# Conv taps queued behind the last low half, copies shared by two engines, later loads of x and fewer pairs by seven in a hybrid decoder layer

## The chip, the cores and the metric

The kernel runs on one core of a Trainium2 chip. The metric is the device time of one execution in microseconds. TensorE (PE) does matmuls, VectorE (DVE) and ScalarE (ACT) elementwise work, GpSimd (POOL) little here; SyncE (SP) issues the loads. The weights stream from HBM through the whole run.

## The reference

One layer on x (256 x 4096) and 256 memory tokens: a projection of x by w_in, whose columns feed three groups, each gated; the groups together go through w_out, and a layer norm closes the layer.

```python
proj = x @ w_in[l]
(c_a, c_b, c_gate, g_q, g_k, g_v, g_lr, g_gate, m_q, m_gate) = jnp.split(proj, split_idx, axis=-1)
y_conv = _conv_group(c_a, c_b, ...) * silu(c_gate)     # h = c_a * sigmoid(c_b); 31-tap causal
                                                       # conv per channel; layer norm; silu
y_gla = _gla_group(g_q, g_k, g_v, g_lr, ...) * silu(g_gate)
y_mem = _memory_group(m_q, mem @ w_mem_kv[l]) * silu(m_gate)
out = concatenate([y_conv, y_gla, y_mem], axis=-1) @ w_out[l]
x = _layernorm(DN_ALPHA * x + out, ln_g[l], ln_b[l])
```

## The kernel before

**Products.** The data is float32; each operand is split into a high half (a cast on ScalarE, L122) and a low half (a subtraction on VectorE, L123) by `halves` (L120). A product takes three matmuls: high by high, high by low, low by high. The halves of x stay in SBUF (`hx`, `lx`); those of the weights (`hiw`, `low`) are made from each loaded chunk (`raww`) just ahead of use. The raw chunks have a ring of three, the halves rings of four tiles; `push` makes a tile and uses the one that was made three tiles earlier.

**Stages, in the order of the run.** Two pairs of conv projections (`cb`, each with its `ca`; about 6 to 97 and 97 to 202 us), memory keys and values (`memory`, L1036, 64 half tiles of 12 matmuls, 202 to 376), the memory queries (`mq`, to 460), two panels of GLA queries (to 550), the keys (`k`, to 632), the values, two pairs of gates (`gg`; the second from 893 to 976), the conv gates (`cg`, to 1062), the memory gates, then the output projection and the norm.

**Pairs by seven.** `pair` (L369) projects onto 1024 columns in 16 chunks of two k-tiles. A chunk by eight makes two tiles of 12 matmuls. A chunk by seven saves one product in eight: VectorE first makes differences of the weights, `tx` (L439) and `ty` (L445, L448), and then four tiles (c, a, y, x) of 3, 6, 6 and 6 matmuls follow. It also needs sums of the halves of x (`sums`, L175: one add L180, five small ones L190, and the halves `eh`, `el`). `BY7` (L50) gives for each pair the pattern of chunks, the blocks of x taken by seven, which sums are made after it is queued, and which are given back.

**Work between the tiles.** After a tile's matmuls `use` first takes one step of `later` (the adds that close the pair before), then `work` (transposes, sums, scores, by `do_work`) and `fill`. In `fill` are the conv's taps (`queue_conv`, L811; the 31 taps of 8 blocks of channels, each one VectorE instruction of 128 x at most 256, L828 and L837): after a pair's chunk as many as `FILLS` says (1 in the second conv pair, else 3), after a half tile of memory `MEM_FILLS` = 5. A transpose (`queue_transpose`, L221) is one VectorE instruction and 16 copies of 32 x 256 on ScalarE (L243). `X_AT` (L32) says with which chunk of the first pair which block of x is loaded; the loads stand with those of the weights on SP's queue.

The order in the code isn't that of the engines: the Tile framework simulates the program and places an instruction on its engine when its operands are ready. A tap needs only the conv's input and the tap ahead of it.

Of the kernel before, what the change touches and what calls it, by code (L numbers as in the profile page):

```python
# [9 lines left out]
F32 = mybir.dt.float32  # L10
# [3 lines left out]
ALU = mybir.AluOpType  # L14
# [5 lines left out]
KT = D // P  # L20
# [10 lines left out]

X_AT = {0: (1,), 1: (2,), 3: (3,), 4: (6,), 5: (4,), 6: (7,), 7: (5,)}  # L32

# [17 lines left out]
    ("cb", 0): ("8888888887878787", (6, 7), (), ()),  # L51
    ("cb", 1): ("8888878787878787", (5, 6, 7), (5,), (5,)),
    ("mq", 0): ("8888888887878787", (6, 7), (), (6, 7)),
    ("k", 0): ("8888878787878787", (5, 6, 7), (5, 6, 7), (5,)),
# [4 lines left out]

FILLS = {("cb", 1): 1}  # L60
MEM_FILLS = 5


@with_exitstack
def layer_kernel(ctx, tc, xT, memT, xres, w_mem, w_in, w_pairs, w_last, cst, w_gate,
                 conv_g, conv_b, norm_g, ln_g, ln_b, out):
    nc = tc.nc
# [52 lines left out]
    def halves(src, hi, lo):  # L120

        nc.scalar.copy(out=hi, in_=src)  # L122
        nc.vector.tensor_tensor(out=lo, in0=src, in1=hi.bitcast(F32), op=ALU.subtract)  # L123

# [34 lines left out]
    work = deque()  # L159
    fill = deque()  # L160
# [60 lines left out]
    def queue_transpose(src, dst, then, back=False):  # L221
# [11 lines left out]
        def moves(b):  # L233
            if b == 0:
                st["d"] = dst()
            tok = "p t (q j c) -> p t q j c"
            feat = "p q (t i c) -> p t q i c"
            flat = "p (q t i c) -> p t q i c" if back else "p (t q j c) -> p t q j c"
            sizes = dict(q=4, t=2, c=32)
            frm = st["t"].rearrange(flat, **sizes)  # L240
            to = st["d"].rearrange(tok if back else feat, c=32, **({"q": 4} if back else {"t": 2}))
            for a in range(4):
                nc.scalar.copy(  # L243
                    out=to[32 * b : 32 * b + 32, :, :, a, :],
                    in_=frm[32 * a : 32 * a + 32, :, :, b, :],
                )
# [48 lines left out]
    def flush():  # L295
        while stream:
            stream.popleft()()


    def panel(chunks, width, stat, then, fills=0, apart=0, soon=KT // 2):  # L300
# [20 lines left out]
        def make(c):  # L321
            if c % 2 == 0:
                raw[0] = w_raw([P, 4, width], "w")
                nc.sync.dma_start(
                    out=raw[0], in_=chunks[c // 2].rearrange("p (k n) -> p k n", k=4)
                )
            w = w_tiles([P, 2, width], "w", KT // 2 - apart <= c < KT // 2 - WBUFS)
            halves(raw[0][:, 2 * (c % 2) : 2 * (c % 2) + 2, :], *w)
            held[c] = w

        def use(c):
# [4 lines left out]
            if c < KT // 2 - apart:  # L336
                for w in held[c]:
                    for tt in range(2):
                        mms(c, tt, w, w is held[c][1])
            if later:  # L340
                later.popleft()()
            do_work(-(-len(work) // max(1, soon - c)))
            for _ in range(min(fills, len(fill))):
                fill.popleft()()

# [23 lines left out]
    def pair(chunks, order, stat, ext, then, soon=KT // 2, fills=0, units=False, beside=None):  # L369
# [41 lines left out]
        def make(n, i):  # L411
# [43 lines left out]
            w = tuple(t[:, : 1 if nm == "c" else 2, :] for t in w_tiles([P, 2, 512], "w"))  # L455
            halves(st[n][nm], *w)
            st[n, nm] = w
# [5 lines left out]
        def use(n, i):  # L463
# [10 lines left out]
            for second in range(2):  # L474
                for j, (slot, stationary, bk) in enumerate(terms):
                    sh, sl = stationary(c)
                    for s in (sh,) if second else (sh, sl):
# [6 lines left out]
                        )  # L484
            if later:
                later.popleft()()
            if i == len(tiles) - 1:
                for _ in range(min(fills, len(fill))):
                    fill.popleft()()
                do_work(-(-len(work) // max(1, soon - n)))  # L490

# [544 lines left out]
    def memory():  # L1036
        m_units, raws, tiles, banks = [], {}, {}, []

        def make(kt, half):
# [8 lines left out]
            tiles[kt, half] = w_tiles([P, 1024], "wm")  # L1048
            halves(raw, *tiles[kt, half])

        def use(kt, half):
# [22 lines left out]
            if half and kt % 4 == 3:  # L1074
                give(mh, ml)
            if later:
                later.popleft()()
            do_work(-(-len(work) // max(1, KT - kt)))
            for _ in range(min(MEM_FILLS, len(fill))):
                fill.popleft()()  # L1080

# [421 lines left out]
```

## Time and profile before

| | |
|---|---|
| time, median of 3 runs | 1538.81 us (1537.97 to 1539.09) |
| the profiled execution | 1540.91 us, of which the span is 1538.9 |
| mean granted TensorE clock | 0.993 of full speed |
| TensorE busy | 1506.4 us (98% of the span), 6809 matmuls |
| VectorE busy | 1210.9 us (79%) |
| ScalarE busy | 901.6 us (59%) |
| chain of work that ended last | TensorE 86%, VectorE 6%, ScalarE 3%, issue 3%, DMA 2% |

Busy time is the time in which an engine had at least one instruction under way; instructions overlap a little, so two starts lie closer together than one instruction is long. The span runs from the first to the last instruction. The granted clock is a share of full speed (2.4 GHz); the lower level is 1.2 GHz.

### The profile page before, as it was taken

What the parts mean: (1) busy time and instruction counts of PE and PEld (TensorE: products, weight loads), DVE (VectorE), ACT (ScalarE), POOL (GpSimd) and SP (SyncE); (2) the same over time, 40 slices, a digit from 0 to 9 for tenths busy, and PEclk for the clock granted to TensorE, in tenths of its full rate; (3) what the DMA queues carried; (4) which work ended last, traced back from release to release, by engine and by line L of the source; (5) the groups of instructions that cost most, each with busy time, mean ns of one, the idle gap of its engine ahead of it and who ended that gap; (6) DMA issues with size and microseconds to landing.
All of it is one profiled execution on the core that took longest, in us unless ns stands there. A gap on an engine that the chain in (4) does not pass through costs nothing.

```text
span 1538.9 us, 18500 instructions
## 1 busy us (share of the span) xinstructions
PE 1506.4 (98%) x6809; PEld 1265.8 (82%) x6809; DVE 1210.9 (79%) x1454; ACT 901.6 (59%) x1203; POOL 49.2 (3%) x59
## 2 busy tenths in 40 slices
PE   8999899999999999999999999999999999999997
PEld 6787678888888888899999887888888887888885
DVE  7799999997686579957575788887757589998955
ACT  6565357438668855676464468577685454555541
POOL 0000000000000000003030000000000000000001
PEclk9999999999999999999999999999999999999998
DMA  8564557765555465555445454656567545565662
GB/s 326 204 219 154 182 172 252 244 206 213 207 189 179 144 238 187 201 197 176 161 156 198 174 213 164 219 218 233 212 219 274 205 178 205 209 216 203 225 223 109
DMA packets 54515, 311.73 MB, mean 203 GB/s; under 512 B 6100, under 2 KB 6484, under 8 KB 27928
## 3 DMA queue, kind: packets, MB, share of 16 engines
q1 hardware_dynamic: 54424, 310.55, 57.1%
q8 instruction: 53, 0.87, 0.2%
q14 instruction: 38, 0.31, 0.1%
HBM read 304.24 MB, written 6.29 MB: 202 GB/s over the span
## 4 chain that ended last, share of the span: by engine, by line
PE 86%; DVE 6%; ACT 3%; issue 3%; DMA 2%; POOL 0%; SPq 0%; DVEq 0%; ACTq 0%
PE acc L478 29%; PE acc L313 28%; PE sm L478 8%; PE acc_N L478 8%; PE mv L1067 6%; PE mk L1067 6%; DVE low L123 2%; DVE cacc L837 2%; ACT S L243 1%; DMA rawx<-xT 1%; DMA raww<-w_in 1%; ACT hiw L122 1%; ACT qkT L243 1%; PE A L749 1%; PE o L274 1%
## 5 line engine op out<-in xcount | busy, mean ns | idle before, releaser
L123 DVE TENSOR_TENSOR low<-raww,hiw 128x1024 fp32r<-128x1024 f32 (+3 forms) x497 | 560.2, 1144 | 171.4 <-ACT hiw L122 139.6
L122 ACT CAST hiw<-raww 128x1024 fp32r<-128x1024 f32 (+3 forms) x497 | 476.7, 978 | 312.9 <-PE acc L313 125.6
L478 PE MATMUL acc<-hiw,hx 128*128 128x512 f32 x528 | 207.7, 393 | 6.1 <-ACT hiw L122 6.1
L313 PE MATMUL acc<-hiw,hx 128*128 128x512 f32 (+2 forms) x576 | 211.8, 368 | 0.1
L313 PE MATMUL acc<-hiw,lx 128*128 128x512 f32 (+2 forms) x576 | 211.7, 368 | 0.0
L478 PE MATMUL acc<-hiw,lx 128*128 128x512 f32 x528 | 206.7, 392 | 0.0
L478 PE MATMUL acc<-low,hx 128*128 128x512 f32 x528 | 169.0, 391 | 6.6 <-DVE low L123 6.6
L313 PE MATMUL acc<-low,hx 128*128 128x512 f32 (+2 forms) x576 | 141.7, 366 | 0.0
L122 ACT CAST hiw<-ty 128x1024 fp32r<-128x1024 f32 x52 | 54.6, 1050 | 130.4 <-DVE ty L448 93.0
L478 PEld LDWEIGHTS acc<-hiw,hx 128*128 128x128 f32 x528 | 100.0, 189 | 29.0 <-ACT hiw L122 8.2
L478 PEld LDWEIGHTS acc<-low,hx 128*128 128x128 f32 x528 | 99.1, 188 | 29.6 <-DVE low L123 9.3
L313 PEld LDWEIGHTS acc<-hiw,hx 128*128 128x128 f32 x576 | 108.2, 188 | 10.9 <-ACT hiw L122 0.4
L478 PEld LDWEIGHTS acc<-hiw,lx 128*128 128x128 f32 x528 | 100.0, 189 | 20.7
L313 PEld LDWEIGHTS acc<-hiw,lx 128*128 128x128 f32 x576 | 108.2, 188 | 10.3
L313 PEld LDWEIGHTS acc<-low,hx 128*128 128x128 f32 x576 | 107.2, 188 | 10.7
L122 ACT CAST hiwm<-rawwm 128x1024 fp32r<-128x1024 f32 x64 | 66.4, 1053 | 73.3 <-PE mv L1067 26.5
L837 DVE SCALAR_TENSOR_TENSOR cacc<-hT,cst_sb,cacc 128x255 f32<-128x255 f32 (+29 forms) x240 | 99.1, 462 | 0.0
L243 ACT COPY S<-T 32x256 f32<-32x256 f32 x224 | 90.3, 403 | 7.0 <-DVE T L229 3.2
L478 PE MATMUL acc<-hiw,xh 128*128 128x512 f32 x224 | 87.4, 390 | 1.6 <-ACT hiw L122 1.6
L123 DVE TENSOR_TENSOR low<-ty,hiw 128x1024 fp32r<-128x1024 f32 x52 | 63.6, 1222 | 31.7 <-ACT hiw L122 21.0
L478 PE MATMUL acc<-hiw,xl 128*128 128x512 f32 x224 | 87.2, 389 | 0.0
L439 DVE TENSOR_TENSOR tx<-raww 128x1024 f32<-128x1024 f32 x52 | 63.4, 1220 | 21.9 <-DMA raww<-w_in 21.8
(268 smaller groups left out, 2529.6 us busy)
## 6 DMA issues: line engine op xcount, KB each, us to landing
raww<-w_in SPq DMA_DIRECT2D x143, 1024.0 KB
raww<-w_pairs SPq DMA_DIRECT2D x48, 1024.0 KB
rawwm<-w_mem SPq DMA_DIRECT2D x64, 512.0 KB
raww<-w_in SPq DMA_DIRECT2D x32, 824.0 KB
raww<-w_last SPq DMA_DIRECT2D x16, 1024.0 KB
raww<-w_in SPq DMA_DIRECT2D x8, 832.0 KB
rawmem<-memT SPq DMA_DIRECT2D x8, 512.0 KB
xr<-xres SPq DMA_DIRECT2D x8, 512.0 KB
```

The lines of the kernel that those rows point to most:

```text
L122: nc.scalar.copy(out=hi, in_=src)
L123: nc.vector.tensor_tensor(out=lo, in0=src, in1=hi.bitcast(F32), op=ALU.subtract)
L243: nc.scalar.copy(out=to[32 * b : 32 * b + 32, :, :, a, :], in_=frm[32 * a : 32 * a + 32, :, :, b, :],)
L274: nc.tensor.matmul(ps, lhsT=a, rhs=b, start=t == 0 and k == 0, stop=t == n - 1 and k == 2)
L313: nc.tensor.matmul(banks[tt][:, :width], lhsT=s[:, kt % 4, tt * P : (tt + 1) * P], rhs=w[:, k, :], start=kt == 0 and not second and s is s ...
L439: nc.vector.tensor_tensor(out=x, in0=raw[:, 3:4, :].to_broadcast([P, 2, 512]), in1=raw[:, 0:3:2, :], op=ALU.subtract,)
L478: nc.tensor.matmul(bank_of(bk), lhsT=s, rhs=w[second][:, slot, :], start=first[bk] == (n, nm, j) and not second and s is sh, stop=last[bk] ...
L749: nc.tensor.matmul(ps[:, at : at + n], lhsT=keys[:, j, k0 : k0 + P], rhs=qs[:, j, q0 : q0 + n], start=dk == 0, stop=dk == 1,)
L837: nc.vector.scalar_tensor_tensor(out=a, in0=h, scalar=dw_sb[:, cb, j : j + 1], in1=a, op0=ALU.mult, op1=ALU.add)
L1067: nc.tensor.matmul(banks[half * 4 + a * 2 + mt], lhsT=s[:, kt % 4, mt * P : (mt + 1) * P], rhs=w[:, 512 * a : 512 * a + 512], start=kt == ...
```

## The change

Four things, in one diff.

- **Taps and work behind the last low half.** `halves` now returns its subtraction; `made[0]` holds the last one. A new function `aside` stands at the end of `use` in panel, pair and memory: it takes one step of `later`, and then issues taps and `work` inside `tc.issue_after(made[0].ins)`, so that the framework places them behind the last low half that was made. `FILLS` gives two taps a chunk to the second conv pair and to the queries, and `MEM_FILLS` falls from 5 to 3.
- **Copies.** Of the 16 copies behind a transpose every other one goes to VectorE.
- **x later.** Blocks 2, 3, 6, 4, 7 and 5 of x are loaded with chunks 2, 4, 5, 6, 7 and 9 of the first pair instead of 1, 3, 4, 5, 6 and 7.
- **Fewer by seven in the queries.** `mq` has two chunks by seven instead of four, of block 7 alone; the sums of x6 are given back before it.

```diff
-X_AT = {0: (1,), 1: (2,), 3: (3,), 4: (6,), 5: (4,), 6: (7,), 7: (5,)}
+X_AT = {0: (1,), 2: (2,), 4: (3,), 5: (6,), 6: (4,), 7: (7,), 9: (5,)}
...
-    ("cb", 1): ("8888878787878787", (5, 6, 7), (5,), (5,)),
-    ("mq", 0): ("8888888887878787", (6, 7), (), (6, 7)),
+    ("cb", 1): ("8888878787878787", (5, 6, 7), (5,), (5, 6)),
+    ("mq", 0): ("8888888788888887", (7,), (), (7,)),
...
-FILLS = {("cb", 1): 1}
-MEM_FILLS = 5
+FILLS = {("cb", 1): 2, ("mq", 0): 2}
+MEM_FILLS = 3
...
-        nc.vector.tensor_tensor(out=lo, in0=src, in1=hi.bitcast(F32), op=ALU.subtract)
+        return nc.vector.tensor_tensor(out=lo, in0=src, in1=hi.bitcast(F32), op=ALU.subtract)
...
-                nc.scalar.copy(
+                f = nc.scalar.copy if a % 2 else nc.vector.tensor_copy
+                f(
...
+    made = [None]
+
+    def aside(n, taps):
+
+
+        if later:
+            later.popleft()()
+        with tc.issue_after(made[0].ins):
+            for _ in range(min(taps, len(fill))):
+                fill.popleft()()
+            do_work(n)
...
-            halves(st[n][nm], *w)
+            made[0] = halves(st[n][nm], *w)
...
-            if later:
-                later.popleft()()
-            if i == len(tiles) - 1:
-                for _ in range(min(fills, len(fill))):
-                    fill.popleft()()
-                do_work(-(-len(work) // max(1, soon - n)))
+            done = i == len(tiles) - 1
+            aside(-(-len(work) // max(1, soon - n)) if done else 0, fills if done else 0)
...
-            if later:
-                later.popleft()()
-            do_work(-(-len(work) // max(1, KT - kt)))
-            for _ in range(min(MEM_FILLS, len(fill))):
-                fill.popleft()()
+            aside(-(-len(work) // max(1, KT - kt)), MEM_FILLS)
```

How the order of the instructions moves is shown at three places. In the rows a name stands with its number, `low` is the low half of a weight tile, `cacc` the conv's running sum.

VectorE in the second conv pair, in a chunk by seven, before:

```order
L123 TENSOR_TENSOR low_1220<-raww_1212,hiw_1219 128x512
L445 TENSOR_TENSOR ty_1215<-raww_1212,tx_1214 128x512
L837 SCALAR_TENSOR_TENSOR cacc_1022<-hT_930,cst_sb,cacc_1022 128x245
L123 TENSOR_TENSOR low_1231<-raww_1212,hiw_1230 128x1024
L837 SCALAR_TENSOR_TENSOR cacc_1022<-hT_930,cst_sb,cacc_1022 128x245 x2
L837 SCALAR_TENSOR_TENSOR cacc_1022<-hT_930,cst_sb,cacc_1022 128x244
L448 TENSOR_TENSOR ty_1215<-raww_1212,ty_1215 128x512
L837 SCALAR_TENSOR_TENSOR cacc_1022<-hT_930,cst_sb,cacc_1022 128x244 x3
L439 TENSOR_TENSOR tx_1294<-raww_1292 128x1024
L837 SCALAR_TENSOR_TENSOR cacc_1022<-hT_930,cst_sb,cacc_1022 128x243 x3
L123 TENSOR_TENSOR low_1247<-ty_1215,hiw_1246 128x1024
```

And the same engine in the same chunk after:

```order
L123 TENSOR_TENSOR low_1207<-raww_1194,hiw_1206 128x1024
L454 TENSOR_TENSOR ty_1219<-raww_1216,tx_1218 128x512
L123 TENSOR_TENSOR low_1224<-raww_1216,hiw_1223 128x512
L842 SCALAR_TENSOR_TENSOR cacc_1022<-hT_969,cst_sb,cacc_1022 128x248
L457 TENSOR_TENSOR ty_1219<-raww_1216,ty_1219 128x512
L123 TENSOR_TENSOR low_1236<-raww_1216,hiw_1235 128x1024
L842 SCALAR_TENSOR_TENSOR cacc_1022<-hT_969,cst_sb,cacc_1022 128x247
L123 TENSOR_TENSOR low_1252<-ty_1219,hiw_1251 128x1024
L842 SCALAR_TENSOR_TENSOR cacc_1022<-hT_969,cst_sb,cacc_1022 128x246
```

Where up to four taps stood between two steps of the weights, one stands behind a low half. In the whole stage there are 85 taps before and 20 after, in the memory stage 163 and 176, in the queries none and 47, in the first q stage none and 5.

ScalarE in the second gate pair, around the casts of `ty` and `tx` in the second chunk by seven after a transpose (`S` is its result, `xh` the high half of that), before:

```order
L122 CAST xh_7702<-S_7681 128x1024
L122 CAST hiw_7663<-ty_7627 128x1024
L243 COPY S_7708<-T_7706 32x2x4x32 x13
L122 CAST hiw_7686<-tx_7626 128x1024
L243 COPY S_7708<-T_7706 32x2x4x32 x3
L122 CAST hiw_7734<-raww_7732 128x1024
```

And after, first ScalarE:

```order
L122 CAST hiw_7659<-tx_7605 128x1024
L122 CAST hiw_7714<-raww_7712 128x1024
L122 CAST hiw_7725<-raww_7712 128x1024
L244 COPY S_7688<-T_7686 32x2x4x32 x8
L122 CAST hiw_7743<-raww_7736 128x512
L122 CAST hiw_7755<-raww_7736 128x1024
```

then VectorE at the same place:

```order
L123 TENSOR_TENSOR low_7715<-raww_7712,hiw_7714 128x1024
L244 COPY S_7688<-T_7686 32x2x4x32 x8
L123 TENSOR_TENSOR low_7726<-raww_7712,hiw_7725 128x1024
L448 TENSOR_TENSOR tx_7738<-raww_7736 128x1024
L123 TENSOR_TENSOR low_7744<-raww_7736,hiw_7743 128x512
L123 TENSOR_TENSOR xl_7706<-S_7688,xh_7705 128x1024
L123 TENSOR_TENSOR low_7756<-raww_7736,hiw_7755 128x1024
L454 TENSOR_TENSOR ty_7739<-raww_7736,tx_7738 128x512
L448 TENSOR_TENSOR tx_7818<-raww_7816 128x1024
L457 TENSOR_TENSOR ty_7739<-raww_7736,ty_7739 128x512
```

The copies no longer stand between the casts of one chunk; eight are on each engine, and `tx` of the following chunk by seven (`tx_7818`) stands ahead of this chunk's `ty`.

VectorE in the keys, where the sums of x5 are made (`f`, then `el`, their low half, which the chunks by seven need), before:

```order
L190 TENSOR_TENSOR f_4671<-r_4670,f_4671 128x2x128
L123 TENSOR_TENSOR low_4529<-raww_4526,hiw_4528 128x1024
L180 TENSOR_TENSOR r_4681<-hx_247,lx_248 128x1024
L123 TENSOR_TENSOR low_4550<-raww_4526,hiw_4549 128x1024
L123 TENSOR_TENSOR el_4678<-f_4671,eh_4677 128x1024
L123 TENSOR_TENSOR low_4568<-raww_4565,hiw_4567 128x1024
L439 TENSOR_TENSOR tx_4605<-raww_4603 128x1024
```

And after:

```order
L190 TENSOR_TENSOR f_4651<-r_4650 128x2x128 x2
L123 TENSOR_TENSOR low_4647<-tx_4585,hiw_4646 128x1024
L190 TENSOR_TENSOR f_4651<-f_4651,r_4650 128x2x128
L123 TENSOR_TENSOR low_4689<-raww_4686,hiw_4688 128x1024
L190 TENSOR_TENSOR f_4651<-r_4650,f_4651 128x2x128
L180 TENSOR_TENSOR r_4661<-hx_281,lx_282 128x1024
L123 TENSOR_TENSOR el_4658<-f_4651,eh_4657 128x1024
```

The first `el` stood ahead of the first `tx`; now it stands behind the last low half of the first chunk by seven (`low_4647`) and the first of the chunk after it (`low_4689`).

## Rows read from the trace of the kernel before

**Rows 1.** The page's busy times: engine, us, share of the span, instructions.

```profile
PE 1506.4 (98%) x6809; PEld 1265.8 (82%) x6809; DVE 1210.9 (79%) x1454; ACT 901.6 (59%) x1203; POOL 49.2 (3%) x59
```

**Rows 2.** Windows by stage: length, busy us (count) of each engine, clock, DMA share, GB/s.

```profile
97.00:201.80 104.80, 93.33 (x376) 71.50 (x374) 101.72 (x160) 56.60 (x71) 0.00 (x0) 0.95 0.52 176
201.80:376.00 174.20, 173.47 (x764) 143.30 (x765) 164.58 (x266) 97.00 (x129) 1.97 (x2) 1.00 0.65 215
376.00:460.00 84.00, 84.00 (x372) 69.54 (x372) 60.15 (x61) 56.92 (x81) 0.00 (x0) 1.00 0.58 213
460.00:505.00 45.00, 45.00 (x219) 38.02 (x218) 27.34 (x31) 37.59 (x73) 0.00 (x0) 1.00 0.50 167
505.00:550.00 45.00, 45.00 (x216) 37.91 (x215) 29.32 (x32) 34.20 (x61) 0.00 (x0) 1.00 0.58 204
550.00:632.00 82.00, 82.00 (x374) 68.33 (x373) 69.01 (x79) 48.69 (x61) 0.00 (x0) 1.00 0.54 191
893.00:976.00 83.00, 80.76 (x348) 65.82 (x347) 69.76 (x73) 59.70 (x82) 0.00 (x0) 0.98 0.54 192
976.00:1062.00 86.00, 85.50 (x376) 69.80 (x375) 71.32 (x73) 59.97 (x84) 0.00 (x0) 1.00 0.61 218
```

**Rows 3.** Windows of 10 us in the second conv pair, same columns.

```profile
130.00:140.00 10.00, 7.40 (x32) 5.53 (x31) 10.00 (x19) 2.66 (x3) 0.00 (x0) 1.00 0.39 116
...
160.00:170.00 10.00, 6.33 (x20) 4.16 (x19) 10.00 (x18) 4.94 (x5) 0.00 (x0) 0.76 0.61 208
...
190.00:200.00 10.00, 6.26 (x20) 4.34 (x19) 10.00 (x20) 6.69 (x8) 0.00 (x0) 0.83 0.61 202
```

**Rows 4.** TensorE's waits over the run: us in total, times, longest us.

```profile
PE acc L478 <- ACT hiw L122: 7.7, 6, 2.5
PE acc L478 <- DVE low L123: 7.0, 7, 2.1
```

**Rows 5.** VectorE's timeline before 195 us: start, us, line, operation, count.

```profile
190.55 1.22 DVE L123 TENSOR_TENSOR low<-raww,hiw 128x1024 fp32r<-128x1024 f32 x1
191.68 1.59 DVE L837 SCALAR_TENSOR_TENSOR cacc<-hT,cst_sb,cacc 128x239 f32<-128x239 f32 x4
193.19 0.69 DVE L448 TENSOR_TENSOR ty<-raww,ty 128x512 f32<-128x512 f32 x1
193.79 1.22 DVE L837 SCALAR_TENSOR_TENSOR cacc<-hT,cst_sb,cacc 128x238 f32<-128x238 f32 x3
```

**Rows 6.** Window from one tx to the second next, columns as in rows 2.

```profile
139.78:166.68 26.90, 22.50 (x90) 15.75 (x89) 26.90 (x45) 11.78 (x14) 0.00 (x0) 0.97 0.55 194
```

**Rows 7.** The same window, taps of L837 alone: VectorE, clock, DMA share, GB/s.

```profile
139.78:166.68 26.90, 10.69 (x26) 0.97 0.55 194
```

**Rows 8.** Groups by line, whole run: count, ns min/median/max, first and last start, shape.

```profile
L243 ACT COPY S<-T x224: 396/403/411, 377.3 to 1194.5; 32x256 f32<-32x256 f32 x112
...
L793 DVE TENSOR_SCALAR ss<-ss x8: 143/150/155, 732.1 to 868.3; 128x1 f32<-128x1 f32 x8
...
L828 DVE TENSOR_SCALAR cacc<-hT,cst_sb x8: 408/408/412, 118.0 to 241.2; 128x256 f32<-128x256 f32 x8
...
L190 DVE TENSOR_TENSOR f<-r x20: 411/417/425, 24.9 to 1287.2; 128x256 f32<-128x256 f32 x20
```

**Rows 9.** TensorE's timeline in the second gate pair, wait in brackets.

```profile
956.08 0.50 PE L478 MATMUL sm<-hiw,eh 128*128 128x512 f32 x1 [2.18 <-ACT hiw L122]
...
958.99 0.63 PE L478 MATMUL acc_N<-hiw,lx 128*128 128x512 f32 x1
959.42 0.63 PE L478 MATMUL acc<-hiw,hx 128*128 128x512 f32 x1
```

**Rows 10.** ScalarE's timeline at the same place.

```profile
949.57 5.39 ACT L243 COPY S<-T 32x256 f32<-32x256 f32 x13 [0.66 <-DVE xl L123]
954.98 1.04 ACT L122 CAST hiw<-tx 128x1024 fp32r<-128x1024 f32 x1
```

**Rows 11.** VectorE's timeline in the first conv pair.

```profile
62.06 1.23 DVE L439 TENSOR_TENSOR tx<-raww 128x1024 f32<-128x1024 f32 x1 [5.79 <-DMA raww<-w_in]
```

**Rows 12.** TensorE's timeline at the same place.

```profile
64.47 0.50 PE L478 MATMUL acc<-low,hx 128*128 128x512 f32 x1 [2.09 <-DVE low L123]
```

More of the change, by code (lines that the diff above doesn't have):

```diff
@@ L327, in make @@
             w = w_tiles([P, 2, width], "w", KT // 2 - apart <= c < KT // 2 - WBUFS)
-            halves(raw[0][:, 2 * (c % 2) : 2 * (c % 2) + 2, :], *w)
+            made[0] = halves(raw[0][:, 2 * (c % 2) : 2 * (c % 2) + 2, :], *w)
             held[c] = w
@@ L339, in use @@
                         mms(c, tt, w, w is held[c][1])
-            if later:
-                later.popleft()()
-            do_work(-(-len(work) // max(1, soon - c)))
-            for _ in range(min(fills, len(fill))):
-                fill.popleft()()
+            aside(-(-len(work) // max(1, soon - c)), fills)
         for c in range(KT // 2):
@@ L484, in use @@
                         )
-            if later:
-                later.popleft()()
-            if i == len(tiles) - 1:
-                for _ in range(min(fills, len(fill))):
-                    fill.popleft()()
-                do_work(-(-len(work) // max(1, soon - n)))
+            done = i == len(tiles) - 1
+            aside(-(-len(work) // max(1, soon - n)) if done else 0, fills if done else 0)
         for n, (_, _, tiles) in enumerate(plan):
@@ L1048, in make @@
             tiles[kt, half] = w_tiles([P, 1024], "wm")
-            halves(raw, *tiles[kt, half])
+            made[0] = halves(raw, *tiles[kt, half])
         def use(kt, half):
@@ L1075, in use @@
                 give(mh, ml)
-            if later:
-                later.popleft()()
-            do_work(-(-len(work) // max(1, KT - kt)))
-            for _ in range(min(MEM_FILLS, len(fill))):
-                fill.popleft()()
+            aside(-(-len(work) // max(1, KT - kt)), MEM_FILLS)
         def done():
```

## The prediction

> **What bounds the kernel now.** I read first the busy times of the page: TensorE is busy for 98% of the span, VectorE for 79% [rows 1]. So only time that TensorE loses can be won, and the question is where it loses it. The windows by stage answer that [rows 2]. In the stage of the queries (376 to 460 us) TensorE never idles: 84.00 us for 372 matmuls, 0.2258 us each, which I take as its rate at full clock. In the stretch from 97 to 201.8 us, the second pair of conv projections, it makes 376 matmuls, which at that rate need 376 x 0.2258 = 84.9 us, in 104.8 us: **19.9 us are lost there**. Some 11.5 of them are idle (104.8 - 93.33 busy), the rest is a lower clock (0.95 over the stretch). The same sum gives 83.0 - 348 x 0.2258 = 4.4 us for the stage at 893 us, 86.0 - 376 x 0.2258 = 1.1 for the one at 976, and nothing in the others shown, but the memory stage: 174.2 - 764 x 0.2258 = 1.7.
>
> Next, who makes TensorE wait in the bad stretch. VectorE is busy for 101.72 of its 104.8 us [rows 2], and in each window of 10 us where TensorE does little, VectorE shows 10.00 of 10 [rows 3]. TensorE's waits over the whole run are for a low half from VectorE and for a high half from ScalarE, seven and six times, 14.7 us together [rows 4]. ScalarE is not busy there; its cast waits for VectorE, which makes the sum ty that is cast. The timeline shows why: four conv taps stand in front of the second half of ty, 1.51 us from their start to its start, so a tap occupies VectorE for 0.38 us; a low half of 1024 columns takes 1.13 from start to start, a half of ty 0.60, each about 0.08 less than its busy time [rows 5]. After the waits at 164 and 192 us the granted clock is at 0.76 and 0.83 [rows 3]: it falls to the lower of its levels for some microseconds, and the matmuls that follow a wait cost nearly twice.
>
> **The second conv pair.** Take two turns of its loop, one chunk by eight and one by seven each, from one tx to the tx two turns on: 26.9 us, 90 matmuls, VectorE busy all through [rows 6], with 26 taps in them [rows 7]. 26 x 0.38 = 9.9 us of taps leaves 17.0, so 8.5 us of VectorE work per turn without taps. TensorE needs 45 x 0.2258 = 10.2. Before, the turn costs VectorE 8.5 + 13 x 0.38 = 13.4, and VectorE sets the time. In the changed order a turn holds four taps: 8.5 + 4 x 0.38 = 10.0, just under TensorE's 10.2. Over the stage 20 taps stand instead of 85: 65 x 0.38 = 24.7 us go. What comes in is one set of sums for x5 (an add and a low half of 1024 columns, four adds of 256 at 417 - 80 ns [rows 8], 2 x 1.13 + 4 x 0.34 = 3.6 us), one low half of memory (1.13) and eight of the moved copies (below, 2.7 us): 7.4. VectorE's load is thus some 101.7 - 24.7 + 7.4 = 84.4 us for 84.9 of TensorE. That is level, and not below it. The best end is no loss, a gain of 19.9. At the worst VectorE is also idle at the start as now (104.8 - 101.7 = 3.1 us), and as much again since it runs ahead to chunks that haven't landed, so that it ends at 84.4 + 6.2 = 90.6 and leaves 5.7 plus a clock that stays low after one wait, 1: a gain of 13. I take a loss of 3 and **a gain of 17**.
>
> **Where the taps go.** The memory stage has 176 taps instead of 163, 16 copies, and one conv norm (14 instructions) less, since that moves behind it. VectorE's 164.58 us there [rows 2] become 164.6 + 13 x 0.38 + 16 x 0.34 - 7 = 168 of 174: it stays below TensorE, and three taps behind each pair of halves (3 x 0.38 + 1.13 = 2.3 us) fit in a tile's 12 matmuls (2.7 us). The tap now waits for the last low half that was made; that is on VectorE itself, so nothing is queued behind that wait that could have gone ahead. Cost 0 to +3, taken as +0.5. In the queries' stage 47 taps and 16 copies come (17.9 + 5.4 us), two pairs of k-tiles by seven go, each with two low halves, a tx and two halves of ty (1.73 + 1.13 + 1.20, so 8.1 for both): 60.15 + 23.3 - 8.1 = 75 of 84.00 us, hidden. The conv's result is first needed by the gate stage at 976 us, so its end may come late. By eight in place of seven costs three matmuls a pair, 6 x 0.2258 = **+1.4**. Five taps, the norm (about 7 us) and 46 copies (15.6) fall into the two q stages, where VectorE has 27.34 and 29.32 of 45 us each [rows 2]: 57 + 25 = 82 of 90, hidden if evenly spread. 0 to +2, taken as +0.5.
>
> **The copies.** Half of the 352 copies behind a transpose, 32x256 each, go from ScalarE (403 ns) to VectorE [rows 8]. No row shows one on VectorE. Bounds: the shortest VectorE instruction here, 150 ns, and a multiply-add of 128x256 with one tensor source, 408 ns; an add of that shape has 417 [rows 8]. I take 0.34 from start to start, the latter less 0.08, as they have the same columns per partition. The Trainium skill has a rule that gives less: "VectorE: DVE Perf Modes", section on the perf-mode tier table, lets a tensor_copy or tensor_scalar on float32 in SBUF run at twice the rate of a two-source operation. The row of the tensor_scalar speaks against it here, 408 against 417 ns; no run here shows the copy. By the rule, at half of 0.34 (an estimate by that page), the sixteen copies in the gate stage would cost 2.7 us less, and the sum would lie 1 to 3 us lower.
>
> **The gate stage at 893 us.** TensorE waits 2.18 us for the cast of tx and then runs on at the lower clock, 0.43 us a matmul [rows 9]. The cast stood behind 13 copies, 5.39 us, on ScalarE [rows 10]. In the new order ScalarE has eight copies there, behind the casts of the chunk, and VectorE the other eight. So that wait goes, up to 4.4 us of it. What is late next: VectorE gets 16 x 0.34 = 5.4 us onto 69.76 of 83 us, and most of it within two turns, where the sevens leave 10.2 - 8.5 = 1.7 us free each; and the tx of the following seven now stands ahead of the low half of this seven's ty, so that it can hold that up until its weights land. Such a case is in the trace: VectorE idle for 5.79 us before a tx whose weights came late, while TensorE waited 2.09 us [rows 11, 12]. Net -4.4 to +3, taken as **-1**. The next stage (976 us) loses its 1.1 us in the same way: -1.1 to +1, taken as -0.5. The wait at 62 us lies where x is loaded beside the weights; with x spread over later chunks the weights come sooner: -2.2 to +1, taken as -1.
>
> **The keys' stage (550 us).** Before, the low half of the sums of x5 stands well ahead of the first seven. Now four adds and that low half (el) stand behind the first low half of the chunk after it. From the moment the ring lets VectorE go on, it has 1.13 + 0.34 + 1.13 + 0.34 + 1.13 + 1.13 = 5.2 us to el, and TensorE 19 matmuls, 4.3 us, that don't need it: a wait of 1 at least. If VectorE has no lead, copies, ty and two adds come on top, and it is 5. Taken as **+2.5** (0 to +5).
>
> The other waits (the start, 1296 us, the tail with its norm) keep their causes: 0.
>
> **The sum.** -17 + 0.5 + 1.4 + 0.5 + 2.5 - 1 - 0.5 - 1 = -14.6 us. Against the profiled execution's 1540.91 that is 1526.3; the median of the runs is 2.1 lower (1538.81), so **1524**. The bounds add up to -26.4 and +2.9; terms that are independent and squared together give about 6 below and 7 above: 1518 to 1531.
>
> **Rivals.** (a) VectorE stays the bound of the second conv pair: load 84.4 against 84.9 is a tie, and each late low half also lowers the clock. Then only some 9 us come back there, and with the other terms it is 1539 - 9 + 2.4 = 1532. For: the tie; against: the turn with four taps has 0.2 us to spare, and the taps stand behind a low half, not in front of ty. 0.12. (b) All comes back and the copies cost 0.15, their lower bound, so that the gate stages lose nothing and the keys and q stages 2 us less: -20 + 1.4 + 1 - 4.4 - 1 - 2 = -25, some 1514. 0.08. (c) Slower: with the taps gone VectorE reaches each tx before its weights have landed and holds up the low halves behind it, as at 62 us, in the sevens of the second conv pair, the keys and the gates, 18 in all. Each costs 2.1 of waiting and about as much in low clock, 4.2. It must happen 4 times to eat the 14.6, and 5 times to be slower by more than 0.2%: at 8 times it is 1524 + 34 = 1558, at 5 it is 1545. For: tx does stand ahead in the new order; against: the keys' and gates' sevens of before have it too and show one wait between them, and the late landing coincided with loads of x. 0.05. (d) The order isn't what the code asks for and taps still crowd in: the new order shows one tap behind a low half, so only an effect that is given back elsewhere leaves it at 1539. 0.04.
>
> **How the numbers follow.** The forecast (1518 to 1531) 0.71, (a) 0.12, (b) 0.08, (c) 0.05, (d) 0.04. The range takes in most of (a) and (b): 1514 to 1534. About 0.2%, 3.1 us, is what a measurement of this kernel can tell from no change. Faster by that: 0.71 + 0.12 + 0.08 less a little for (a)'s tail, 0.89; within it 0.05; slower 0.06.
>
> **What would show it.** In the profile after: the stretch of the second conv pair lasts some 86 to 90 us, at a granted clock of 0.99 or 1, its VectorE below its full share with about 20 taps. The copy of 32x256 on VectorE at 0.25 to 0.42 us. No wait for the cast of tx in the gate stage. A wait of 1 to 5 us in the keys' stage before el. The memory stage stays at 174 us with VectorE near 168. It is wrong if VectorE is still busy all through the conv pair, or if waits for low or for tx's weights appear at several of the sevens.

## The result and the profile after

The changed kernel takes 1521.77 us (median of 4 runs, 1520.85 to 1522.14) against 1538.95 of the kernel before beside it: a ratio of 0.9887, 95% interval 0.987 to 0.9904, 17.2 us less. The forecast was 1524, between 1514 and 1534. The profiled execution took 1522.14 us (before 1540.91), its span is 1520.4, the granted clock 0.996.

The page's busy times and its chain, answering to [rows 1] and to the table of before:

```profile
PE 1498.6 (99%) x6815; PEld 1265.1 (83%) x6815; DVE 1258.5 (83%) x1620; ACT 834.0 (55%) x1023; POOL 49.2 (3%) x59
...
PE 95%; DVE 2%; DMA 2%; ACT 0%; issue 0%; SPq 0%; POOL 0%; DVEq 0%; ACTq 0%
```

VectorE has 48 us more to do than before and ScalarE 68 less, yet the chain that ended last passes through VectorE for 2% instead of 6% and through ScalarE not at all. The windows by stage, answering to [rows 2] (second conv pair, memory, queries, the two q panels together, keys, second gate pair; same columns):

```profile
97.00:183.00 86.00, 84.83 (x373) 69.61 (x372) 82.88 (x108) 53.16 (x62) 0.00 (x0) 1.00 0.61 208
183.00:357.00 174.00, 174.00 (x769) 144.11 (x769) 169.83 (x290) 82.89 (x93) 0.00 (x0) 1.00 0.65 215
357.00:443.00 86.00, 86.00 (x381) 71.24 (x380) 73.21 (x107) 47.20 (x59) 0.00 (x0) 1.00 0.57 197
...
443.00:531.00 88.00, 88.00 (x423) 74.22 (x422) 75.12 (x125) 61.87 (x105) 1.97 (x2) 1.00 0.58 205
...
531.00:615.00 84.00, 82.44 (x371) 67.39 (x370) 73.36 (x89) 45.21 (x53) 0.00 (x0) 1.00 0.52 180
870.00:957.00 87.00, 83.66 (x362) 68.51 (x361) 77.13 (x92) 55.08 (x69) 0.00 (x0) 0.98 0.53 189
```

The second conv pair now lasts 86.0 us for 373 matmuls, which at 0.2258 us need 84.2: 1.8 are lost there, not 19.9. Its clock is 1.00. The memory stage, the queries and the q panels, which took over the taps and the conv's end, show TensorE busy from end to end, with VectorE up to 169.83 of 174. New losses stand in the keys (TensorE busy for 82.44 of 84.00) and in the second gate pair (87.0 - 362 x 0.2258 = 5.3).

To compare many runs I use one sum for all of them: of each two matmuls in a row whose starts lie more than 0.26 us apart, the distance less 0.227 (the usual one), added up between 20 and 1490 us of the span and by place. It holds idle time and lower clock together. All numbers in us. The sums are those of the profiled execution, the time is the median (the profiled execution lies 2.0 us above it for before, 2.7 for e5 and 2.5 for e10, and 1.7 below it for e7). The column of the second conv pair reaches into the first microseconds of the memory stage; of the 20.6 of before, 1.0 lies there.

| run | at 62 us | second conv pair | memory, queries, q | keys | second gate pair | conv gates | all | time |
|---|---|---|---|---|---|---|---|---|
| before | 2.4 | 20.6 | 0 | 0 | 4.4 | 1.1 | 33.3 | 1538.9 |
| changed | 0 | 1.6 | 0 | 2.7 | 5.4 | 0 | 14.6 | 1521.8 |
| e1 nothing pinned | 1.3 | 19.4 | 2.0 | 0 | 0.8 | 2.0 | 30.7 | 1538.2 |
| e2 only taps pinned | 2.0 | 1.7 | 0 | 0 | 0.7 | 1.1 | 10.4 | 1518.0 |
| e3 copies on ScalarE | 0 | 3.9 | 5.1 | 3.3 | 3.9 | 4.7 | 25.6 | 1533.4 |
| e4 x as before | 0 | 1.6 | 0 | 2.7 | 5.6 | 0 | 14.9 | 1522.6 |
| e5 taps pinned, copies on ScalarE | 0.7 | 2.4 | 4.9 | 0 | 4.3 | 2.3 | 20.2 | 1527.4 |
| e6 before, one tap | 0 | 1.0 | 0 | 0 | 4.2 | 1.1 | 13.6 | 1519.8 |
| e7 taps and sums of x5 pinned | 0 | 1.5 | 0 | 0 | 0.8 | 0 | 7.5 | 1516.6 |
| e8 and taps moved on | 0 | 0 | 0.8 | 0 | 0.7 | 0.8 | 7.7 | 1515.7 |
| e9 five taps a half tile | 0 | 1.6 | 24.3 | 2.3 | 5.2 | 0 | 37.9 | 1545.3 |
| e10 five taps, buffers kept | 0 | 1.5 | 15.9 | 2.4 | 5.5 | 0 | 32.1 | 1537.0 |
| e11 before, copies shared | 1.4 | 18.2 | 0 | 0 | 0 | 1.2 | 26.0 | 1533.6 |

The start (some 2 us at 24 us, about 4 in e6 and e10) and the output projection (1.5 to 3) are in "all" alone. From before to changed the sum falls by 18.7, and six more matmuls cost 1.4: 17.3. The medians differ by 17.2; the two profiled executions, from which the sums come, by 18.8, so some 1.5 us between them lie outside the sum. "Pinned" stands for issued behind the last low half.

### The profile page after: what moved, and what is told of

Same layout as the page of the kernel before. It is cut to its first block, busy times and chain, and to the rows that moved or that the text cites. A ratio compares the mean times of both kernels' runs of the same rounds, so it can differ in the third digit from the quotient of the medians.

```text
span 1520.4 us, 18486 instructions
## 1 busy us (share of the span) xinstructions
PE 1498.6 (99%) x6815; PEld 1265.1 (83%) x6815; DVE 1258.5 (83%) x1620; ACT 834.0 (55%) x1023; POOL 49.2 (3%) x59
## 4 chain that ended last, share of the span: by engine, by line
PE 95%; DVE 2%; DMA 2%; ACT 0%; issue 0%; SPq 0%; POOL 0%; DVEq 0%; ACTq 0%
PE acc L487 34%; PE acc L326 29%; PE acc_N L487 9%; PE sm L487 9%; PE mk L1072 6%; PE mv L1072 6%; DMA raww<-w_in 2%; DVE low L123 1%; PE A L754 1%; PE o L275 1%; PE sc L275 0%; PE mo L275 0%; DVE xr L1265 0%; ACT hiw L122 0%; SPq L149 0%
## 5 line engine op out<-in xcount | busy, mean ns | idle before, releaser
L487 PEld LDWEIGHTS acc<-hiw,hx 128*128 128x128 f32 x536 | 101.0, 188 | 26.4 <-ACT hiw L122 5.7
L326 PEld LDWEIGHTS acc<-hiw,lx 128*128 128x128 f32 x576 | 108.2, 188 | 10.4
L326 PEld LDWEIGHTS acc<-low,hx 128*128 128x128 f32 x576 | 107.1, 188 | 10.4
L842 DVE SCALAR_TENSOR_TENSOR cacc<-hT,cst_sb,cacc 128x239 f32<-128x239 f32 (+27 forms) x240 | 101.9, 463 | 0.6
L123 DVE TENSOR_TENSOR lowm<-rawwm,hiwm 128x1024 fp32r<-128x1024 f32 x64 | 77.7, 1220 | 2.4 <-ACT hiwm L122 1.5
L487 PE MATMUL acc<-low,xh 128*128 128x512 f32 x224 | 71.7, 389 | 0.2 <-DVE low L123 0.2
```

The lines of the kernel that those rows point to most:

```text
L123: return nc.vector.tensor_tensor(out=lo, in0=src, in1=hi.bitcast(F32), op=ALU.subtract)
L326: nc.tensor.matmul(banks[tt][:, :width], lhsT=s[:, kt % 4, tt * P : (tt + 1) * P], rhs=w[:, k, :], start=kt == 0 and not second and s is s ...
L487: nc.tensor.matmul(bank_of(bk), lhsT=s, rhs=w[second][:, slot, :], start=first[bk] == (n, nm, j) and not second and s is sh, stop=last[bk] ...
L842: nc.vector.scalar_tensor_tensor(out=a, in0=h, scalar=dw_sb[:, cb, j : j + 1], in1=a, op0=ALU.mult, op1=ALU.add)
```

## The experiments

**e1: nothing pinned.** The changed kernel with `aside` as

```diff
-        with tc.issue_after(made[0].ins):
-            for _ in range(min(taps, len(fill))):
-                fill.popleft()()
-            do_work(n)
+        for _ in range(min(taps, len(fill))):
+            fill.popleft()()
+        do_work(n)
```

> The changed kernel, but taps and work are issued freely again, not behind the last low half; the numbers of taps, the copies, the loads of x and the pairs by seven stay as changed. Its order has 81 taps in the second conv pair instead of 20, and the sums of x5 stand early in the keys as before. Theory (the taps behind the low halves carry the gain): the second conv pair loses some 18 us again, its VectorE is busy all through; the keys' wait of 2.6 us goes: 1522 + 18 - 2.6 = 1537, between 1533 and 1541. Rival (the copies, the loads and the fewer pairs by seven carry it): 1520 to 1527.

1538.17 us (ratio to before 0.9994, 0.9985 to 1.0003): as slow as before, with all the other parts of the change in. The window of the second conv pair:

```profile
97.00:200.00 103.00, 90.83 (x375) 71.92 (x374) 102.47 (x163) 53.41 (x62) 0.00 (x0) 0.95 0.53 178
```

VectorE is busy for 102.47 of 103 us again, with 81 taps in that window (before 85, changed 20). Without the pin the numbers in `FILLS` and `MEM_FILLS` don't keep the taps out of that pair; the framework places them where VectorE is ready for them. This run frees taps and work together; e2 tells the two apart.

**e6: the taps away.** The kernel before, in which the loop over the taps makes only the first of 31 (`for j in (TAPS - 1,)`).

> The kernel before with only the first of the 31 taps of each block of channels (the conv is left out but for that tap). Theory (taps on VectorE are the whole loss in the second conv pair): TensorE has no wait for low halves or casts there, the stretch lasts 85 to 88 us, and all else stays as before: 1539 - 18 = 1521, between 1518 and 1524. Rival (weights that land late or casts hold that pair too): 5 us or more stay lost there, 1526 or more.

1519.83 us (ratio 0.9881, 0.9867 to 0.9894), the second conv pair in 86 us with 1.0 left:

```profile
97.00:183.00 86.00, 85.27 (x376) 70.18 (x375) 75.14 (x82) 62.15 (x86) 0.00 (x0) 1.00 0.62 214
```

So the taps were the loss in that pair, all but a microsecond of it; neither weights nor casts hold it. Its VectorE needs 75 us without them; between that and TensorE's 85 there is room for some 25 taps of 0.38 us, and the change puts 20 there.

**e4: the loads of x.** The changed kernel with the `X_AT` of before.

> The changed kernel with x loaded with the chunks of before. Theory: the wait of 2.1 us at about 62 us is there again, with VectorE idle before tx for weights that come late, and nothing else changes: 1524, between 1522.5 and 1526. Rival (that wait went for another reason): 1521 to 1522.5, no wait at 62 us.

1522.57 us (0.9898, 0.9885 to 0.9912), no wait at 62 us: the rival's side, and my reason for that wait fell. The loads hardly move: in both traces the last load of x goes out at 16 us (16.1 in the changed kernel, 15.9 here), among the first chunks, and the one clear difference is a pair of loads at about 5 us, one of x and one of weights, that stands the other way round.

**e2: only the taps pinned.** `do_work(n)` moved out of the `with`.

> The changed kernel, but only the taps are issued behind the last low half; transposes, sums and other work are free. Theory: the second conv pair stays cured (20 taps), the wait of 1.6 us at 174 us goes since the sums of x5 leave that stage, the 2.6 us in the keys go since the sums stand early again, and of the 5 us in the second gate pair half or more goes since tx of the following chunk no longer stands between the halves of ty: 1522 - 1.3 - 2.6 - 2.5 = 1516, between 1513 and 1520. Rival (work that is free crowds in front of low halves again and brings other waits): 1522 to 1527.

1518.0 us (0.9868, 0.9855 to 0.9882), 3.8 less than the changed kernel. The keys wait for nothing, and the second gate pair loses 0.7 instead of 5.4. VectorE there, with TensorE's last matmul ahead of its wait, first of the changed kernel and then of e2:

```profile
943.78 0.68 DVE L454 TENSOR_TENSOR ty<-raww,tx 128x512 f32<-128x512 f32 x1
944.69 1.23 DVE L448 TENSOR_TENSOR tx<-raww 128x1024 f32<-128x1024 f32 x1 [0.23 <-DMA raww<-w_in]
945.83 0.68 DVE L457 TENSOR_TENSOR ty<-raww,ty 128x512 f32<-128x512 f32 x1
...
944.25 0.40 PE L487 MATMUL sm<-low,hx 128*128 128x512 f32 x1
```

```profile
942.47 0.68 DVE L457 TENSOR_TENSOR ty<-raww,ty 128x512 f32<-128x512 f32 x1
943.89 1.22 DVE L448 TENSOR_TENSOR tx<-raww 128x1024 f32<-128x1024 f32 x1 [0.74 <-DMA raww<-w_in]
945.03 1.22 DVE L123 TENSOR_TENSOR low<-ty,hiw 128x1024 fp32r<-128x1024 f32 x1
...
943.58 0.39 PE L487 MATMUL sm<-low,hx 128*128 128x512 f32 x1
```

In the changed kernel the tx of the following chunk stands between the halves of ty, in e2 ty is done first. Against that last matmul (944.25 us, and 943.58 in e2) the second half of ty starts 1.6 us later in the one and 1.1 us earlier in the other. What the expectation missed: the wait at 62 us came back, though x is loaded as in the changed kernel:

```profile
61.58 1.23 DVE L448 TENSOR_TENSOR tx<-raww 128x1024 f32<-128x1024 f32 x1 [5.36 <-DMA raww<-w_in]
```

With e4 that points to the work: free, the sums of x5 stand in the first conv pair. The other wait that the expectation saw going, the one at 174 us, stayed as well (1.7 in the table).

**e7: the sums of x5 pinned too.** As e2, and in the second conv pair

```diff
-                    work.append(lambda u=u: extX.update({u: sums(*x_units[u])}))
+                    work.append(lambda u=u, k=key: late(u) if k == ("cb", 1) else extX.update({u: sums(*x_units[u])}))
```

where `late` makes the sums inside `tc.issue_after(made[0].ins)`.

> Only the taps and, in the second conv pair, the sums of x5 are issued behind the last low half; other work is free; copies shared as changed. Theory (the wait at 62 us went in the changed kernel because the sums of x5 left the first conv pair, not because of the loads of x): that wait of 2.1 us is gone, the keys and the second gate pair stay without their waits: 1518 - 2 = 1516, between 1514.5 and 1517.5. Rival (the sums only move the wait into the second conv pair, whose VectorE is nearly full): 1518 to 1520, with waits there of over 2 us.

1516.64 us (0.9859, 0.9846 to 0.9873), no wait at 62 us. The time alone doesn't tell it from e2, whose interval overlaps; the trace does. The seven traces in which the sums of x5 stand outside the first conv pair show no wait at 62 us, and five of the six with them inside show one, of 0.7 to 2.4 us. The sixth is e6: the low half of the sums stands there at 52.01 us, and yet TensorE doesn't wait. So the place of the sums brings the wait about, but not alone. The load queue's own waits tell a part: between 30 and 70 us it stands for 17.0 us until adds of the sums are done in e2, for 8.5 in e7, and the last two loads of weights ahead of that tx go out at 54.51 and 56.25 us instead of 51.85 and 54.73. In e6 they go out no earlier (54.99 and 57.38), but tx starts at 59.87 us, not 61.58. Why the weights landed sooner there stays open.

**e8: taps moved on.** As e7, with `FILLS` 1 in the second conv pair and 3 in the queries.

> As the run with taps and the sums of x5 behind the low half, and with one tap a chunk instead of two in the second conv pair (10 instead of 20) and three instead of two in the queries (61 instead of 47). Theory (the 1.5 us left in the second conv pair are VectorE's load): that wait halves or goes, the queries have VectorE at some 79 of 86 us and wait for nothing: 1516 - 1 = 1515, between 1513.5 and 1516.5. Rival (the taps cost in the queries what they gave back): 1517 or more.

1515.67 us (0.9856, 0.9843 to 0.987). The 1.5 us in the second conv pair go, and 0.8 come in a q panel. That the 1.5 were VectorE's load isn't shown by it. In the changed kernel the cast of ty there stands on ScalarE behind a copy of `ca`, which waits for TensorE:

```profile
174.28 0.59 ACT L1015 COPY ca<-acc 128x512 f32<-128x512 f32 x1 [1.68 <-PE acc L487]
174.76 1.05 ACT L122 CAST hiw<-ty 128x1024 fp32r<-128x1024 f32 x1
```

VectorE had that ty done at 173.81 us. In e8 this copy comes only at 177.92 us, and the cast starts 0.1 us after its ty is done. At 1515.45 to 1516.6 against 1514.91 to 1517.02, e7 and e8 can't be told apart; both beat the changed kernel by 5 to 6 us.

**e3: all copies on ScalarE.** `f = nc.scalar.copy` for every copy, the rest as changed.

> The changed kernel, but all copies behind a transpose are on ScalarE as before. Theory: the conv pair needs no copies on VectorE, it stays cured; in the second gate pair 16 copies (6.6 us) stand on ScalarE ahead of the cast of ty, a wait of 2 to 5 us in place of the 3.3 now: 1522, between 1519 and 1525. Rival (relief of ScalarE is part of the gain): 1528 or more, with waits for casts in several stages.

1533.36 us (0.9966, 0.9953 to 0.9978): the rival. The theory had the second conv pair right but not the rest; 11.6 of the 17.2 us hang on the shared copies. TensorE's waits, and ScalarE in the queries:

```profile
PE acc L487 <- ACT hiw L122: 10.7, 7, 2.8
```

```profile
394.95 6.62 ACT L244 COPY S<-T 32x256 f32<-32x256 f32 x16
401.59 2.00 ACT L122 CAST hiw<-raww 128x1024 fp32r<-128x1024 f32 x2
```

Pinned work puts all 16 copies of a transpose in one row, 6.6 us, in front of a cast that TensorE needs. So it is at four places, about 401, 512, 953 and 1040 us, and TensorE loses 2 to 5 us at each. At two more, at 165 and 597 us, it loses 2 with no copies in front: there the cast waits for ty from VectorE.

**e5: taps pinned, work free, copies on ScalarE.** e2 and e3 together, to see whether the pinned work is the whole of it.

> The kernel of the run in which only the taps are issued behind the last low half, but with all copies on ScalarE. Theory (copies on ScalarE cost 11.6 us only because work that is issued behind the last low half stands there 16 in a row, 6.6 us, ahead of casts): free work spreads them between the casts as before, so only the wait in the second gate pair comes back, 2 to 4 us: 1518 + 2.5 = 1520.5, between 1518 and 1523. Rival (ScalarE needs the relief whatever the order): 1528 to 1533, with waits for casts in several stages.

1527.37 us (0.993, 0.9917 to 0.9944), between the two: 6 us better than e3, 9.4 worse than e2. Half of these 9.4 (4.9 us) stand at 508 to 518 us in the q panels; 3.6 stand in the second gate pair, which loses 4.3 again, as before. ScalarE over both panels, of e5 and then of e2, and its timeline in e5:

```profile
443.00:531.00 88.00, 85.13 (x401) 71.20 (x400) 60.43 (x78) 79.24 (x152) 1.97 (x2) 0.98 0.54 183
```

```profile
443.00:531.00 88.00, 88.00 (x424) 74.26 (x423) 78.37 (x129) 62.51 (x105) 1.97 (x2) 1.00 0.61 213
```

```profile
508.71 4.96 ACT L244 COPY qkT<-T 32x256 f32<-32x256 f32 x12
513.70 1.04 ACT L122 CAST hiw<-raww 128x1024 fp32r<-128x1024 f32 x1
```

ScalarE is busy for 79.24 of 88 us (before 37.59 and 34.20 of 45 each, [rows 2]) and makes 96 copies there instead of 80; the late taps bring the conv's end, with its transposes, towards the stages where ScalarE already copies for the queries.

**e11: the copies alone.** The kernel before with every other copy on VectorE.

> The kernel before with one part of the change alone: every other copy behind a transpose is on VectorE. Theory (the shared copies are worth much only once the taps come late, so that the conv's end and its copies meet those of the queries on ScalarE; in the kernel before only the second gate pair waits for them): the 4.4 us there go, the second conv pair still loses some 20 us: 1539 - 4 = 1535, between 1533 and 1539. Rival (ScalarE's relief is worth its 9 to 12 us by itself): 1527 to 1531.

1533.56 us (0.9966, 0.9953 to 0.9979), 5.4 less than before: the second gate pair's 4.4, and by the table 2.4 in the second conv pair and 1.0 at 62 us. So the copies are worth 5 alone and 9 to 12 beside late taps, and the second conv pair still loses 18.2 with them. (e1 has the copies too; it gives 1.4 back in six more matmuls, 2.0 in a wait at 458 us and 2 more in the second conv pair and the conv gates.)

**e9: five taps a half tile.** The changed kernel with `MEM_FILLS = 5`.

> The changed kernel with five taps behind each half tile of memory instead of three. Its order has 228 taps in the memory stage instead of 176 and none in the queries; the keys have their sums early. Theory (a stage is free of loss as long as VectorE's own load in it is below TensorE's): three taps and a low half take 3 x 0.38 + 1.13 = 2.3 us of a half tile's 2.7, five take 3.0; VectorE's load in the stage is 169.8 measured + 52 x 0.38 + 8 x 0.29 + the conv norm of 7 = 199 minus its present slack, 174 - 169.8 = 4: some 15 to 20 us are lost there, less 2.7 in the keys: 1522 + 15 = 1537, between 1530 and 1542. Rival (behind the low half a tap costs nothing, since the next low half is already made): 1519 to 1524.

1545.33 us (1.0041, 1.0027 to 1.0055), slower than before. The size is larger than I worked out and its form is another: up to 288 us TensorE loses nothing, and then one wait of 21.5 us comes, with 2.6 more behind it at the lower clock. The window up to there (columns as before), the wait, and VectorE:

```profile
183.00:288.00 105.00, 105.00 (x465) 87.00 (x464) 104.59 (x182) 49.30 (x53) 0.00 (x0) 1.00 0.66 219
...
PE mk L1072 <- DVE lmem L123: 21.5, 1, 21.5
```

```profile
289.74 19.38 DVE L842 SCALAR_TENSOR_TENSOR cacc<-hT,cst_sb,cacc 128x231 f32<-128x231 f32 x51
309.04 1.23 DVE L229 STREAM_TRANSPOSE T<-cacc 128x1024 f32<-128x1024 f32 x1
310.20 1.17 DVE L123 TENSOR_TENSOR lmem<-rawmem,hmem 128x1024 fp32r<-128x1024 f32 x1
```

In the first 105 us VectorE is full (104.59, 122 taps where the changed kernel has 109), and TensorE is busy all through. Then 51 taps stand in a row ahead of the low half of a block of memory tokens. The code hands out its 32 buffers in the order in which it is written: with five taps a tile the conv's last tap is written early, its two buffers go to the next block of memory tokens, and that block waits for every tap still to come.

**e10: the conv's buffers kept to the end of the memory stage.**

```diff
-            give(st["hT"])
+            give_late(st["hT"])
```

and the same for the conv's sum; `give_late` holds both until `done` of the memory stage.

> As the run with five taps behind each half tile of memory, but the conv's two buffers are given back only at the end of the memory stage, not when its last tap is issued, so that no block of memory tokens is loaded into them. Its order has 186 taps in the memory stage, none 51 in a row, and 42 in the queries. Theory (the 21.5 us wait came from a block of memory tokens that had to wait for a buffer of the conv, and with it for all its taps): that wait is gone: 1522, between 1518 and 1526. Rival (five taps a tile are simply more than VectorE can do beside the low halves): 1533 to 1546, spread over many waits in the memory stage.

1537.04 us (0.9987, 0.9977 to 0.9997). The time lies where the rival had it, but not for the rival's reason, and the theory was right for the memory stage alone:

```profile
183.00:357.00 174.00, 174.00 (x770) 144.04 (x769) 171.35 (x297) 82.87 (x92) 0.00 (x0) 1.00 0.67 219
```

TensorE is busy all through it beside 194 taps. That is only 9 more than the changed kernel has in the same stretch, so this run doesn't try the load that e9 had in mind; what it shows is that the wait of 21.5 us is gone once the buffers are kept. One wait, 12.5 us, moved behind the stage, with 3.3 at the lower clock:

```profile
PE sm L494 <- DVE mvl L123: 12.5, 1, 12.5
```

It is for the low half of the memory values, and while it waits VectorE works through the conv's norm. By the code's order of buffers one of these low halves gets the buffer that a result of the conv had; no run took that one away too.

## Why the prediction was right, and where it was not

- **What bounds the kernel, and the second conv pair.** Right. The load was worked out as 84.4 us of VectorE against 84.9 of TensorE; measured are 82.88 in 86.00. The 3 us left as a loss are 1.6, so by the table the term is -19 rather than -17 (-18 by the prediction's own sum, 19.9 - 1.8). e1 and e2 show that pinning the taps is what does it, e6 that the taps were the loss. Rival (a), VectorE still the bound, fell; in windows of 10 us like those of [rows 3] VectorE is as full as before, and TensorE doesn't wait. Its one wait of the stage comes later, and e8 above tells what stands in front of it:

```profile
150.00:160.00 10.00, 10.00 (x45) 8.28 (x45) 10.00 (x13) 5.69 (x6) 0.00 (x0) 1.00 0.58 205
160.00:170.00 10.00, 10.00 (x46) 8.26 (x45) 10.00 (x13) 6.64 (x7) 0.00 (x0) 1.00 0.75 254
...
175.86 0.50 PE L487 MATMUL acc<-hiw,hx 128*128 128x512 f32 x1 [1.17 <-ACT hiw L122]
```

- **The other rivals.** (b) fell with the price of the copies, 0.30 and not 0.15, and with the 5.4 us lost in the second gate pair. (c) asked for tx that waits for weights at five sevens or more; of TensorE's losses at the sevens those at 174 and 569 us have other causes, and the one at 948 has 0.23 us of it. (d) fell with 20 taps in the trace.
- **Memory, queries, q panels.** Right: 0.5 and 0.5 were taken, 0 measured. VectorE has 169.83 us in the memory stage where 168 were worked out, 73.21 in the queries (75), 75.12 in the q panels (82).
- **The copies.** The price was too high: 0.34 taken, 0.30 from start to start (eight in 2.36 us, the last 0.28 long); neither 0.17, which the prediction set beside it, nor 0.15 was measured. The step that failed is larger: the prediction counts the copies as a cost to VectorE everywhere and as a gain in the two gate stages alone. e3 and e5 show that without them the pinned work and the late conv take back 9 to 12 us. The forecast came out well since both parts were in the change.
- **The keys.** Right in mechanism and size: +2.5 taken, 2.7 measured. El stands where the new order put it (behind four small adds; the section on the kernel before says five). TensorE's two longest waits there are not for el itself but for a low half that stands among the adds, then for `eh`, which ScalarE casts when the last add is done:

```profile
568.82 0.73 PE L487 MATMUL acc_N<-low,hx 128*128 128x512 f32 x2 [0.75 <-DVE low L123]
570.23 0.50 PE L487 MATMUL acc<-hiw,eh 128*128 128x512 f32 x1 [0.68 <-ACT eh L122]
```

- **The second gate pair.** Mechanism right, size and sign wrong: -1 taken, +1.0 measured (4.4 to 5.4). The wait for the cast of tx behind 13 copies [rows 9, 10] went, and another came:

```profile
947.98 0.79 PE L487 MATMUL acc<-hiw,hx 128*128 128x512 f32 x1 [3.34 <-ACT hiw L122]
```

```profile
946.88 1.05 ACT L122 CAST hiw<-ty 128x1024 fp32r<-128x1024 f32 x1 [6.17 <-DVE ty L457]
```

  ScalarE had been idle for 6.17 us before that cast, since ty came late: eight copies (2.36 us) and the next tx stand ahead of it on VectorE. The prediction named both; it priced the copies as a load on the stage, where they count as a delay of one step. What each adds wasn't measured by itself, but the same copies with free work cost little here: nothing in e11, 0.7 in e2. So it is their place and that of tx that count, and the pinned work sets it.
- **The wait at 62 us.** -1 taken, -2.4 measured, for another reason: not the loads of x (e4), but the sums of x5 that left the first conv pair (e2, e7), with the open end that e6 leaves. The diff says "later", and the order of the loads shows almost no move; I didn't look at that queue's order.
- **The conv gates.** -0.5 taken, -1.1 measured. The copies, which the prediction gave as the reason, don't do it by themselves: e11 still has 1.2 there, e2 1.1 and e7 0. The cause is open.
- **Fewer pairs by seven.** +1.4 taken, and 6815 instead of 6809 matmuls are on the page. It wasn't tried by itself, so the price is counted in matmuls and not measured.

The terms sum to -19.0 + 0 + 1.4 + 2.7 + 1.0 - 1.1 - 2.4 = -17.4 against the -14.6 forecast. The bulk was read off the right stage; of the small terms two had the wrong cause or sign, and their errors, +2.0 and -1.4, nearly cancelled. That is luck. The bounds as listed add up to -26.2 and +3.4, not to -26.4 and +2.9; the forecast doesn't hang on it.

## What to carry to other kernels

Where a framework places ready instructions itself, a number in the code that says how many fillers go between two steps may decide little (85 taps for 1 a chunk, 81 for 2) until the fillers are tied to a step of the main work. Tie other work only where a run shows that it helps: tying all of it cost 3.8 us here, since some of it is needed early, and tying one set of sums took a wait of 2.0 us away. Work out for each stage what every engine has to do and move fillers to where that is below the engine that bounds; then look at what stands ahead of each single step, because a stage with time to spare still waits when eight copies and one more step stand in front of what a cast needs. Filler that ends early in the code can hand its buffers to work that then waits for all of it: five taps instead of three cost 24 us, 21.5 of them in a single wait, in a stage that had shown none.

## What the runs showed of the hardware

The same copy of 32 x 256 takes 403 ns on ScalarE and 284 on VectorE (groups by line of the changed kernel; ns are min/median/max):

```profile
L244 ACT COPY S<-T x112: 400/403/408, 361.6 to 1195.3; 32x256 f32<-32x256 f32 x112
L244 DVE COPY S<-T x112: 271/284/289, 363.2 to 1202.3; 32x256 f32<-32x256 f32 x112
```

The two-source add of 256 columns takes 417 and the shortest instruction 150 [rows 8]. If those 150 are taken as the part that doesn't grow with the columns (an estimate), half of the rest makes 150 + (417 - 150) / 2 = 283. That agrees with the rule of the Trainium skill which the prediction weighed ("VectorE: DVE Perf Modes", section on the perf-mode tier table: a float32 copy in SBUF runs at twice the rate of a two-source operation). It is the length of one instruction, though. What a row of them costs VectorE is told by the distance of their starts:

```profile
565.41 0.75 DVE L190 TENSOR_TENSOR f<-r 128x256 f32<-128x256 f32 x2
936.24 2.36 DVE L244 COPY S<-T 32x256 f32<-32x256 f32 x8
```

Two adds start 0.33 us apart (0.75 - 0.417), eight copies 0.30 ((2.36 - 0.284) / 7): the add's successor starts before the add has ended, the copy's doesn't. So a copy that is a third shorter saves a tenth, and a price should be read from start to start. The row that I set against it, the multiply-add with one tensor source at 408 ns, speaks only for that instruction; why it isn't faster no run here tells.

A wait's price is not its length alone. In the changed kernel the matmuls behind the wait at 947.98 us run 0.43 us apart for some seven of them, at the lower of the clock's levels, which costs 1.9 us beside the wait; behind the one of 1.17 us at 175.86 they run 0.23 apart. In the kernel before, the matmuls behind the wait of 2.18 us at 956 run 0.23 apart at first and 0.43 from 958.99 us on [rows 9], while those behind the wait of 2.09 at 64 us [rows 12] stay at 0.23.
